# A hybrid encoder on one core: the second hyena's filters move from attention into a feed-forward layer

## The chip, the cores and the metric

The program runs on one core of one Trainium2 chip. The metric is device time in microseconds (us), the median of the runs shown. TensorE is called PE, VectorE DVE, ScalarE ACT, GpSimd POOL and SyncE SP, as in the profile.

## What is computed

An encoder of four layers over 512 tokens of 1024 channels. Each layer adds a mixer and then a gated feed-forward network to the residual `x`; the mixers are hyena, window attention, pool, hyena.

```python
for i in range(DEPTH):                      # 4
    kind, s = i % N_MIXERS, i // N_MIXERS   # hyena, attention, pool, hyena
    h = rmsnorm(x, norm_mix[i])
    ...
    x = x + y
    x = x + swiglu(rmsnorm(x, norm_ffn[i]), ff_w_gate[i], ff_w_up[i], ff_w_down[i])

def hyena_filters(L, w1, b1, wi, bi, w3, freq):
    ...                                     # h: sine layers of the positions
    h = h @ w3.astype(f32)
    h = h.reshape(L, 2, HY_ORDER, D) * decay[:, None, None, :]
    fwd, bwd = h[:, 0], h[:, 1]
    k = jnp.concatenate([fwd, jnp.zeros((1, HY_ORDER, D), f32), bwd[1:][::-1]], axis=0)
    return k / jnp.sum(jnp.abs(k), axis=0, keepdims=True)

def window_attention(xn, w_qkv, q_gain, k_gain, sink, w_o, rel_table):
    ...                                     # 16 heads, 4 key heads, blocks of 128, 3 blocks seen
    logits = jnp.where(mask[None, :, None, None], logits + bias, -1e30)
    m = jnp.maximum(jnp.max(logits, axis=-1, keepdims=True), sink_l)
    pr = jnp.exp(logits - m)
    pr = pr / (jnp.sum(pr, axis=-1, keepdims=True) + jnp.exp(sink_l - m))
    o = jnp.einsum('bnkgqs,bnskd->bnqkgd', pr.astype(vw.dtype), vw)
    return o.reshape(B, L, N_HEADS * HEAD_DIM) @ w_o
```

The filters depend on positions and weights alone, not on `x`, so those of the second hyena (layer 3) can be made at any time before it.

## The kernel before, in words

The residual lies channel-major, eight tiles `x` of 128 channels by 512 tokens. Every projection splits both operands into a high and a low part in fp32r and adds three matmuls of 512 columns (`mm3`, lines 206 to 208). `wload` fetches a weight block of 512 KB on SP's queue into `raw`; ACT makes its high part (`hi`, line 191) and DVE the rest (`lo`, line 192), with two `raw` and five `hi` and `lo` buffers.

PSUM has two pools: `mm`, four tiles of one bank, and `aux`, two tiles of two banks. A feed-forward layer (`ffn`) makes 22 blocks of hidden channels, two at a time: the gate sums in `mm`, the up sums in `aux`; then the down projection in two halves of eleven weight blocks, each half with four sums.

A hyena filter is made for an order `o` and 256 channels `q`, eight tiles for a hyena. `filter_time` multiplies the sine features by `w3` (lines 388, 389), by the decay, and takes absolute values; `filter_spectrum` makes the odd part of a discrete transform (line 430), the norm and the tap at time zero in `filter_norm` (lines 413 to 417), then the even part (line 440), joins them, and stores the tile to DRAM (`kd`, lines 450, 451), where the second hyena reads it. `filters` is a generator that yields after each piece. The first hyena's are made among its input projections.

Attention (`attention`) has 32 units: a key head, a block of 128 queries, two of its four heads. `qkv` makes the queries, keys and values in three groups; normalised queries are transposed by PE into `aux` tiles (line 834) and split. For each unit `scores` makes the products of queries and keys (lines 891, 892), adds the bias and takes the maximum on DVE (line 894), and the exponential on ACT (line 902); `turn` transposes (line 915) and copies (`pr`, line 917); `mix_values` multiplies by the values (line 928) and scales (line 930); `put_values` transposes the result back (line 936). The loop holds three units in flight, and between units takes a piece or two of `filters(1, ...)`.

A scheduler sets the final order on each engine from the order of the code, from priorities, and from when buffers of the pools come free; each engine then runs its instructions in that order.

## Time and profile before

| what | us |
|---|---|
| median of 3 runs | 2426.8 (2426.11 to 2430.69) |
| profiled execution | 2429.84 |
| its span | 2428.1 |
| PE busy in it | 2365.2 (97%) |
| DVE busy | 1446.8 (60%) |
| ACT busy | 978.2 (40%) |

The profiled execution is one of its own; what it takes beyond its span lies outside the records. Matmuls overlap in the records, so PE's busy time is not its work: distances from start to start show that. The attention units stand between 817.6 us (first scores) and 992.2 us (first matmul of the output projection); the feed-forward layer after the pool mixer fills 1440 to 1790 us and a little on both sides.

### The profile page before, as it was taken

To read this page: it belongs to the slowest core of one execution; us is meant where nothing else is said; L and a number is where in the kernel's file an instruction comes from. 1 tells how busy PE (TensorE), PEld (TensorE's weight loads), DVE (VectorE), ACT (ScalarE), POOL (GpSimd) and SP (SyncE) were. 2 spreads that over 40 slices of the span, in tenths; PEclk is the share of its full clock that TensorE was granted. 3 is DMA by queue.
4 is the path that set the end of the run, shared out by engine and by line. 5 is a ranking of instruction groups with operands and counts; after the bars stand their busy time and mean duration, and the time that the engine had idled before them with its cause. 6 is when DMAs were issued, how large, how long until landed. Compare 5 with 4: busy or idle time off the path is not lost.

```text
span 2428.1 us, 29260 instructions
## 1 busy us (share of the span) xinstructions
PE 2365.2 (97%) x10966; PEld 1951.1 (80%) x10966; DVE 1446.8 (60%) x2411; ACT 978.2 (40%) x1793; POOL 76.9 (3%) x210
## 2 busy tenths in 40 slices
PE   7999989999999899999999989999989999999999
PEld 5778878878887778888888878888878888888887
DVE  7879886454335798554443365544349997544432
ACT  6543325333234677443332363333234443333321
POOL 0210000000001021000000000000000000000000
PEclk9999999999999899999999999999999999999999
DMA  5342223433334132233332222332232222333332
GB/s 155 130 165 87 96 70 95 110 96 96 96 96 117 57 111 83 91 93 99 100 96 96 86 90 89 101 97 96 96 129 97 96 90 76 96 98 100 97 106 85
DMA packets 176833, 240.42 MB, mean 99 GB/s; under 512 B 8097, under 2 KB 137137, under 8 KB 174516
## 3 DMA queue, kind: packets, MB, share of 16 engines
q1 hardware_dynamic: 174852, 234.27, 30.0%
q0 software_dynamic: 1840, 4.29, 1.0%
q8 instruction: 86, 1.41, 0.2%
q14 instruction: 55, 0.45, 0.1%
HBM read 218.51 MB, written 20.02 MB: 98 GB/s over the span
## 4 chain that ended last, share of the span: by engine, by line
PE 60%; ACT 1%; DVE 1%; issue 0%; ACTq 0%
PE mm L206 10%; PE mm L207 10%; PE mm L208 10%; PE aux L208 7%; PE aux L207 7%; PE aux L206 7%; PE aux L711 1%; PE aux L662 1%; PE mm L928 1%; PE aux L708 1%; PE mm L999 0%; PE aux L430 0%; PE mm L634 0%; PE aux L440 0%; PE aux L653 0%; PE aux L654 0%
## 5 line engine op out<-in xcount | busy, mean ns | idle before, releaser
L192 DVE TENSOR_TENSOR lo<-raw,hi 128x512 fp32r<-128x512 f32 x700 | 483.3, 691 | 705.4 <-ACT hi L191 701.6
L191 ACT CAST hi<-raw 128x512 fp32r<-128x512 f32 x700 | 434.7, 622 | 1013.5 <-PE mm L207 647.6
L206 PE MATMUL mm<-ghs,hi 128*128 128x512 f32 x1168 | 460.8, 396 | 4.2 <-ACT ghs L517 4.2
L208 PE MATMUL mm<-ghs,lo 128*128 128x512 f32 x1168 | 460.3, 394 | 0.0
L207 PE MATMUL mm<-gls,hi 128*128 128x512 f32 x1104 | 435.4, 394 | 0.0
L208 PE MATMUL aux<-ghs,lo 128*128 128x512 f32 x704 | 274.3, 390 | 1.1 <-DVE lo L192 1.1
L206 PE MATMUL aux<-ghs,hi 128*128 128x512 f32 x704 | 274.3, 390 | 0.0
L207 PE MATMUL aux<-gls,hi 128*128 128x512 f32 x704 | 273.9, 389 | 0.0
L206 PEld LDWEIGHTS mm<-ghs,hi 128*128 128x128 f32 x1168 | 220.7, 189 | 54.2 <-ACT ghs L517 4.8
L208 PEld LDWEIGHTS mm<-ghs,lo 128*128 128x128 f32 x1168 | 220.1, 188 | 46.0 <-issue 1.2
L207 PEld LDWEIGHTS mm<-gls,hi 128*128 128x128 f32 x1104 | 208.2, 189 | 45.1 <-issue 2.5
L208 PEld LDWEIGHTS aux<-ghs,lo 128*128 128x128 f32 x704 | 132.1, 188 | 30.2 <-DVE lo L192 2.9
L207 PEld LDWEIGHTS aux<-gls,hi 128*128 128x128 f32 x704 | 132.2, 188 | 27.4
L206 PEld LDWEIGHTS aux<-ghs,hi 128*128 128x128 f32 x704 | 132.2, 188 | 27.1
L206 PE MATMUL mm<-hh,hi 128*128 128x512 f32 x352 | 137.0, 389 | 0.0
L208 PE MATMUL aux<-hh,lo 128*128 128x512 f32 x352 | 137.0, 389 | 0.0
L207 PE MATMUL mm<-hl,hi 128*128 128x512 f32 x352 | 137.0, 389 | 0.0
L206 PE MATMUL aux<-hh,hi 128*128 128x512 f32 x352 | 136.9, 389 | 0.0
L208 PE MATMUL mm<-hh,lo 128*128 128x512 f32 x352 | 136.9, 389 | 0.0
L207 PE MATMUL aux<-hl,hi 128*128 128x512 f32 x352 | 136.9, 389 | 0.0
L296 DVE TENSOR_TENSOR t<-aux,rstd 128x512 f32<-128x512 f32 x88 | 60.5, 687 | 61.9 <-PE aux L208 61.9
L300 ACT CAST hh<-t 128x512 fp32r<-128x512 f32 x88 | 54.6, 620 | 103.2 <-DVE t L297 103.1
(272 smaller groups left out, 3440.5 us busy)
## 6 DMA issues: line engine op xcount, KB each, us to landing
raw<-in_ff_w_gate SPq DMA_DIRECT2D x88, 512.0 KB
raw<-in_ff_w_up SPq DMA_DIRECT2D x88, 512.0 KB
raw<-in_ff_w_down SPq DMA_DIRECT2D x88, 512.0 KB
raw<-in_hy_w_in SPq DMA_DIRECT2D x48, 512.0 KB
kd<-k SPq DMA_DIRECT2D x32, 512.0 KB
kt<-kd SPq DMA_DIRECT2D x16, 1024.0 KB
raw<-in_hy_w_out SPq DMA_DIRECT2D x16, 512.0 KB
raw<-in_at_w_qkv SPq DMA_DIRECT2D x12, 512.0 KB
```

The source lines that it names most:

```text
L191: nc.scalar.copy(hi, raw[:, k:k + step])
L192: nc.vector.tensor_tensor(lo, raw[:, k:k + step], hi.bitcast(F32), op=ALU.subtract)
L206: mm(ps, ah, bh, start=first, stop=False)
L207: mm(ps, ah, bl, start=False, stop=False)
L208: mm(ps, al, bh, start=False, stop=last)
L296: nc.vector.tensor_tensor(t2, u[e], rstd, op=ALU.mult)
L300: nc.scalar.copy(a, t2)
L662: mm(ps[:, j, e], fwd[:, e, r0 + j], u[:, r0 + j], start=e == 0, stop=e == 1)
L708: mm(y[:, r], w, v, start=st, stop=sp)
L711: mm(y[:, e, r * P:(r + 1) * P], v[:, e * P:(e + 1) * P], w, start=st, stop=sp)
L928: nc.tensor.matmul(out, prs[j][:, b * P:(b + 1) * P], self.v[:, k, g * HD:(g + 1) * HD], start=b == 0, stop=b == len(kb) - 1)
```

## The change

The second hyena's filters are no longer made in attention. A new generator, `late_filters`, makes them for 128 channels at a time, 16 half-tiles in place of 8 tiles, and yields six times for each. The feed-forward layer with index 2 (after the pool mixer) takes one piece after each of the gate and up weight blocks from the second pair of hidden blocks on, and three pieces after each block of the down projection. Their sums stand in `mm` tiles of one bank, and half a tile is stored at a time. In attention the scores of a unit's two heads take the two banks of one `aux` tile instead of two `mm` tiles, and of the two copies in `turn` the second goes to DVE.

```diff
@@ -271,6 +271,7 @@
         self.gx_split(lambda k: self.g_ffn(i, k))
         with self.tc.tile_pool(name=f"ffn{i}", bufs=2) as fp, self.tc.tile_pool(name=f"side{i}", bufs=1) as sp:
             side = self.early(sp) if i == 0 else iter(())
+            late = self.late_filters(1, sp) if i == 2 else iter(())
             hh, hl = [], []
             for j in range(0, NF, 2):
                 g = [self.tl(self.mm, [P, L], "mm") for _ in range(2)]
@@ -284,6 +285,8 @@
                                 c = slice(e * P, (e + 1) * P)
                                 self.mm3(ps[e], ws[k][0][:, c], ws[k][1][:, c], self.gh[k0 + k], self.gl[k0 + k],
                                          k0 + k == 0, k0 + k == KD - 1)
+                        if j:
+                            next(late, None)
                 if j == 0:
                     rstd = self.rstd_row(nc.vector)
                 else:
@@ -311,8 +314,9 @@
                     for k, j in self.order(2, 4, half == 1 and k0 + 2 == NF):
                         c = slice(j * P, (j + 1) * P)
                         a, b = hh[k0 + k], hl[k0 + k]
-                        st, sp = k0 + k == 0, k0 + k == NF - 1
-                        self.mm3(ps[j], ws[k][0][:, c], ws[k][1][:, c], a, b, st, sp)
+                        self.mm3(ps[j], ws[k][0][:, c], ws[k][1][:, c], a, b, k0 + k == 0, k0 + k == NF - 1)
+                    for _ in range(3):
+                        next(late, None)
                 with self.tc.high_priority(offset=XP):
                     for j in range(4):
                         xk = self.x[4 * half + j]
@@ -487,6 +491,91 @@
                 yield
             yield from pieces(self.filter_spectrum(fp, s, o, q, *made, fwd, neg))
             made = nxt
+            yield
+
+    def late_filters(self, s, fp):
+
+        nc, t = self.nc, self.t
+        n = GS // 2
+        one = lambda tag, shape, dt=F32, bufs=1: self.tl(fp, shape, tag, dt, bufs)
+        fwd, neg = one("fwd", [P, 2, R, P]), one("neg", [P, 2, P])
+        nc.sync.dma_start(neg, t["dft_neg"])
+        nc.sync.dma_start(fwd, t["dft_fwd"])
+        C, S = lambda r: fwd[:, 0, r], lambda r: fwd[:, 1, r]
+        odd = [[[(C(1), 1), (C(3), 3)], [(S(1), 1), (S(3), 3)]],
+               [[(neg[:, 0], 1), (S(3), 3)], [(C(1), 1), (neg[:, 1], 3)]]]
+        wl = one("w3l", [P, 2, n], F32R)
+        nc.gpsimd.memset(wl[FW:P].bitcast(F32), 0.0)
+        w3 = t["hy_f_w3"][s].rearrange("p (b c) -> p b c", b=2)
+        hh = self.hh[s]
+        for q in range(NG):
+            for o in range(2):
+                self.kd[s, o, q] = self.dr.tile([P, 4, 2, GS], F32, tag=f"kd{s}{o}{q}", name=f"kd{s}{o}{q}")
+        for q, e, o in [(q, e, o) for q in range(NG) for e in range(2) for o in range(2)]:
+            c0 = q * GS + e * n
+            if o == 0:
+                dec = one("dec", [P, R, n])
+                nc.sync.dma_start(dec, t["decay"][:, :, c0:c0 + n])
+            wf = one("w3", [P, 2, n])
+            for d in range(2):
+                nc.sync.dma_start(wf[d * FW:(d + 1) * FW], w3[:, :, o * D + c0:o * D + c0 + n])
+            fb = one("fb", [1, n])
+            nc.sync.dma_start(fb, t["hy_f_bias"][s, o:o + 1, c0:c0 + n])
+            ws = one("w3s", [P, 2, n])
+            nc.vector.tensor_tensor(ws[:, 0], wf[:, 0], wf[:, 1], op=ALU.add)
+            nc.vector.tensor_tensor(ws[:, 1], wf[:, 0], wf[:, 1], op=ALU.subtract)
+            wh = one("w3h", [P, 2, n], F32R)
+            nc.scalar.copy(wh, ws)
+            nc.vector.tensor_tensor(wl[0:FW], ws[0:FW], wh[0:FW].bitcast(F32), op=ALU.subtract)
+            yield
+            ab = one("ab", [P, R, 2, n])
+            mx = one("mx", [P, 2, n])
+            for r0 in (1, 0):
+                ps = self.tl(self.mm, [P, 2, 2, n], "mm")
+                for j in range(2):
+                    c = slice((2 * j + r0) * P, (2 * j + r0 + 1) * P)
+                    nc.tensor.matmul(ps[:, j], hh[:, c], wh, start=True, stop=False)
+                    nc.tensor.matmul(ps[:, j], hh[:, c], wl, start=False, stop=True)
+                nc.vector.tensor_tensor(ab[:, r0::2], ps, dec[:, r0::2].unsqueeze(2).broadcast_to([P, 2, 2, n]), op=ALU.mult)
+                if not r0:
+                    t0 = one("t0", [1, n])
+                    nc.vector.tensor_tensor(t0, ab[0:1, 0, 0], ab[0:1, 0, 1], op=ALU.add)
+                    nc.scalar.mul(ab[0:1, 0], t0.unsqueeze(1).broadcast_to([1, 2, n]), 0.5)
+                ax = one("k4", [P, 2, 2, n], bufs=2)
+                nc.scalar.activation(ax, ab[:, r0::2], AF.Abs)
+                dst = mx if r0 else ax[:, :, 0]
+                nc.vector.tensor_tensor(dst, ax[:, :, 0], ax[:, :, 1], op=ALU.max)
+                yield
+            nc.gpsimd.tensor_tensor(mx, mx, dst, op=ALU.add)
+            nc.gpsimd.tensor_tensor(mx[:, 0], mx[:, 0], mx[:, 1], op=ALU.add)
+            po = self.tl(self.mm, [P, 2, 2, n], "mm")
+            for ty in range(2):
+                for d in range(2):
+                    for m, (w, r) in enumerate(odd[ty][d]):
+                        nc.tensor.matmul(po[:, ty, d], w, ab[:, r, d], start=m == 0, stop=m == 1)
+            od = one("k4", [P, 2, 2, n], bufs=2)
+            nc.scalar.copy(od, po)
+            yield
+            pn = self.tl(self.mm, [P, L], "mm")
+            nc.tensor.matmul(pn[:, n:n + 1], mx[:, 0], self.ones, start=True, stop=True)
+            nc.vector.reciprocal(self.rn[s][q][:, o, e:e + 1], pn[:, n:n + 1])
+            nc.tensor.matmul(pn[0:1, :n], self.ones, mx[:, 0], start=True, stop=True)
+            tap = one("t0", [1, n])
+            nc.vector.tensor_tensor(tap, pn[0:1, :n], fb, op=ALU.mult)
+            nc.vector.tensor_tensor(ab[0:1, 0, 0], ab[0:1, 0, 0], tap, op=ALU.add)
+            yield
+            pe = self.tl(self.mm, [P, 2, 2, n], "mm")
+            for j in range(2):
+                for d in range(2):
+                    nc.tensor.matmul(pe[:, j, d], fwd[:, d, 2 * j], ab[:, 2 * j, d], start=True, stop=True)
+            e2 = one("e2", [P, 2, n])
+            nc.scalar.copy(e2, pe[:, 1])
+            ka, kb = ab[:, 0:2], ab[:, 2:4]
+            nc.vector.tensor_tensor(ka[:, 0], pe[:, 0], e2, op=ALU.add)
+            nc.vector.tensor_tensor(ka[:, 1], pe[:, 0], e2, op=ALU.subtract)
+            nc.vector.tensor_tensor(kb, ka, od, op=ALU.subtract)
+            nc.vector.tensor_tensor(ka, ka, od, op=ALU.add)
+            nc.sync.dma_start(self.kd[s, o, q][:, :, :, e * n:(e + 1) * n], ab)
             yield
 
 
@@ -747,8 +836,6 @@
                 nc.gpsimd.memset(kl[HD:P].bitcast(F32), 0.0)
             ol = [self.tl(a1, [P, 2, L], "ol", F32R)] + qs[0:3]
             self.ol = [a[:, e] for a in ol for e in range(2)]
-            fwd = self.tl(a1, [P, 2, R, P], "fwd")
-            neg = self.tl(a1, [P, 2, P], "neg")
             units = [(g, n, e) for g in range(NKV) for n in range(NB) for e in range(2)]
             made, put = {}, {}
             with ExitStack() as inner:
@@ -760,10 +847,6 @@
                     for _ in self.qkv(i, qp, a1):
                         for j in range(2):
                             made[j] = self.scores(ap, *units[j])
-                fp = inner.enter_context(self.tc.tile_pool(name="fil1", bufs=2))
-                steps = self.filters(1, fp, fwd, neg, 0)
-                for _ in range(2):
-                    next(steps)
                 n = len(units)
                 for j in range(n + 3):
                     if 2 <= j < n:
@@ -774,10 +857,6 @@
                         made[j - 1] = self.turn(ap, *made[j - 1])
                     if 0 <= j - 3:
                         self.put_values(*units[j - 3], put.pop(j - 3))
-                    for _ in range(5 * (j + 1) // 4 - 5 * j // 4):
-                        next(steps, None)
-                for _ in steps:
-                    pass
             self.project(t["at_w_o"][0], self.gh, self.ol, self.natural)
 
     def qkv(self, i, ap, a1):
@@ -845,6 +924,7 @@
         if not self.ready:
             self.ready = True
             yield from self.bias_rows(pool)
+            self.rn[1] = [self.tl(self.per, [P, 2, GS // P], f"rn1{q}") for q in range(NG)]
             yield from self.filter_features(pool, self.per, self.mm, 1)
 
     def bias_rows(self, pool):
@@ -885,8 +965,9 @@
         bias = self.bias[g][e]
         m = self.tl(ap, [P, 4], "m", bufs=4)
         s = []
+        both = self.tl(self.aux, [P, 2, L], "aux")
         for j in range(2):
-            ps = self.tl(self.mm, [P, L], "mm")
+            ps = both[:, j]
             q, k = self.q[h0 // 2][:, j, n * P:(n + 1) * P], (g // 2, g % 2)
             nc.tensor.matmul(ps[:, :w], q, self.kh[k[0]][:, k[1], k0:k0 + w], start=True, stop=False)
             nc.tensor.matmul(ps[:, :w], q, self.kl[k[0]][:, k[1], k0:k0 + w], start=False, stop=True)
@@ -914,7 +995,7 @@
             for b in range(len(kb)):
                 nc.tensor.transpose(pt[:, b * P:(b + 1) * P], s[j][:, b * P:(b + 1) * P], self.ident)
             pr = self.tl(ap, [P, 3 * P], "pr", bufs=4)
-            nc.scalar.copy(pr[:, :w], pt[:, :w])
+            (nc.vector.tensor_copy if j else nc.scalar.copy)(pr[:, :w], pt[:, :w])
             pts.append(pt)
             prs.append(pr)
         return kb, pts, prs, den
```

Outside attention's units and this feed-forward layer the order on every engine is as before. Three places follow. A row is a line of the code (the changed kernel has its own numbers), the instruction, out<-in with buffer numbers, and its size; "x2" merges rows.

**The start of attention, PE.** `qh` are normalised queries (their transposes go to `aux`), `kh`, `kl` and `q` keys and queries in scores. Before:

```order
L834 MATMUL aux_1235_6271<-ident_16_87,qh1_1232_6262 128x128
L834 MATMUL aux_1236_6282<-ident_16_87,qh1_1232_6262 128x128
L936 MATMUL mm_1297_6499<-ident_16_87,o_1278_6432 128x128
L891 MATMUL mm_1305_6528<-kh0_1068_5516,q0_1064_5512 128x384
L892 MATMUL mm_1305_6528<-kl0_1070_5518,q0_1064_5512 128x384
L928 MATMUL mm_1293_6487<-v_1063_5511,pr_1294_6491 128x64 x3
L928 MATMUL mm_1295_6493<-v_1063_5511,pr_1296_6497 128x64
L834 MATMUL aux_1235_6271<-ident_16_87,qh2_1233_6265 128x128
L834 MATMUL aux_1236_6282<-ident_16_87,qh2_1233_6265 128x128
L928 MATMUL mm_1295_6493<-v_1063_5511,pr_1296_6497 128x64 x2
L834 MATMUL aux_1235_6271<-ident_16_87,qh3_1234_6268 128x128
```

Now, the last of the transposes on PE and what follows them:

```order
L913 MATMUL aux_1238_6304<-ident_16_87,qh0_1231_6259 128x128
L913 MATMUL aux_1238_6304<-ident_16_87,qh1_1232_6262 128x128
L913 MATMUL aux_1238_6304<-ident_16_87,qh2_1233_6265 128x128
L913 MATMUL aux_1238_6304<-ident_16_87,qh3_1234_6268 128x128
L972 MATMUL aux_1244_6328<-kh0_1072_5520,q0_1068_5516 128x384
L973 MATMUL aux_1244_6328<-kl0_1074_5522,q0_1068_5516 128x384
L972 MATMUL aux_1255_6364<-kh0_1072_5520,q1_1069_5517 128x384
L973 MATMUL aux_1255_6364<-kl0_1074_5522,q1_1069_5517 128x384
```

The scores of the third unit (384 columns, `q0`) and of later ones stood ahead of and among the 32 transposes of the last four query tiles; now all 32 stand ahead of the third unit.

**Inside attention, PE.** `w3h`, `w3l`, `ab` and `mx` belong to the filters, `lg` and `pr` to `turn` and `mix_values`. Before:

```order
L388 MATMUL aux_1337_6637<-w3h_1321_6582,hh_814_4084 128x512
L389 MATMUL aux_1337_6637<-w3l_1243_6324,hh_814_4084 128x512
L891 MATMUL mm_1416_6907<-kh0_1068_5516,q2_1066_5514 128x384
L892 MATMUL mm_1416_6907<-kl0_1070_5518,q2_1066_5514 128x384
L430 MATMUL aux_1355_6700<-ab_1260_6377,fwd_1073_5523 128x256 x4
L430 MATMUL aux_1355_6700<-ab_1260_6377,neg_1074_5524 128x256
L430 MATMUL aux_1355_6700<-ab_1260_6377,fwd_1073_5523 128x256 x2
L430 MATMUL aux_1355_6700<-ab_1260_6377,neg_1074_5524 128x256
L413 MATMUL aux_1370_6754<-ones_9_80,mx_1268_6403 128x1 x2
```

Now, on PE at such a place, there are units alone:

```order
L996 MATMUL mm_1371_6779<-ident_16_87,lg_1354_6713 128x128 x3
L972 MATMUL aux_1389_6840<-kh0_1072_5520,q2_1070_5518 128x256
L973 MATMUL aux_1389_6840<-kl0_1074_5522,q2_1070_5518 128x256
L996 MATMUL mm_1373_6785<-ident_16_87,lg_1355_6717 128x128 x3
L1017 MATMUL mm_1375_6791<-ident_16_87,o_1358_6728 128x128
L972 MATMUL aux_1377_6796<-kh0_1072_5520,q3_1071_5519 128x384
L973 MATMUL aux_1377_6796<-kl0_1074_5522,q3_1071_5519 128x384
L1009 MATMUL mm_1371_6779<-v_1067_5515,pr_1372_6783 128x64 x3
L1009 MATMUL mm_1373_6785<-v_1067_5515,pr_1374_6789 128x64 x3
```

The filter matmuls are gone, and about one pair of scores and one result's transpose stand between a unit's transposes and its products with the values.

**The down projection, PE and DVE.** `hh` and `hl` are hidden blocks, `hi` and `lo` weight parts. Before, PE had projection matmuls alone:

```order
L206 MATMUL aux_2756_13230<-hh6_2533_12103,hi_2775_13337 128x512
L207 MATMUL aux_2756_13230<-hl6_2534_12104,hi_2775_13337 128x512
L208 MATMUL aux_2756_13230<-hh6_2533_12103,lo_2776_13338 128x512
L206 MATMUL mm_2757_13231<-hh6_2533_12103,hi_2775_13337 128x512
L207 MATMUL mm_2757_13231<-hl6_2534_12104,hi_2775_13337 128x512
L208 MATMUL mm_2757_13231<-hh6_2533_12103,lo_2776_13338 128x512
```

Now, at the same place on PE, a half-tile's tap sum (1x128) and even spectrum (`fwd`) stand among them; its norm stands two matmuls ahead of these rows:

```order
L562 MATMUL mm_2722_13248<-mx_2709_13179,ones_9_80 1x128
L206 MATMUL aux_2687_13077<-hh6_2380_11633,hi_2732_13282 128x512
L207 MATMUL aux_2687_13077<-hl6_2381_11634,hi_2732_13282 128x512
L208 MATMUL aux_2687_13077<-hh6_2380_11633,lo_2733_13283 128x512
L206 MATMUL mm_2688_13078<-hh6_2380_11633,hi_2732_13282 128x512
L570 MATMUL mm_2724_13255<-ab_2708_13178,fwd_2263_11059 128x128 x4
```

On DVE there stand at this place (`rn11` is the norm, `t0` the tap, `ab` what the even spectrum reads):

```order
L547 TENSOR_TENSOR k4_2714_13198<-k4_2714_13198 128x2x128
L561 RECIPROCAL rn11_707_3563<-mm_2722_13248 128x1
L192 TENSOR_TENSOR lo_2760_13417<-raw_2758_13414,hi_2759_13416 128x512
L564 TENSOR_TENSOR t0_2723_13252<-mm_2722_13248,fb_2700_13136 1x128
L565 TENSOR_TENSOR ab_2708_13178<-ab_2708_13178,t0_2723_13252 1x128
L574 TENSOR_TENSOR ab_2708_13178<-mm_2724_13255,e2_2725_13260 128x256
```

Four projection matmuls lie between the tap sum (1x128) and the even spectrum, which reads the sum of `ab` and the tap; a weight split stands on DVE between the norm and the tap. Ten of the 16 half-tiles lie in the down projection in this way; the other six lie among the gate and up blocks, with 22 matmuls at that point.

## Rows read from the trace of the kernel before

**Rows 1.** The page: busy us by engine; one costly group, with its mean ns.

```profile
PE 2365.2 (97%) x10966; PEld 1951.1 (80%) x10966; DVE 1446.8 (60%) x2411; ACT 978.2 (40%) x1793; POOL 76.9 (3%) x210
...
L192 DVE TENSOR_TENSOR lo<-raw,hi 128x512 fp32r<-128x512 f32 x700 | 483.3, 691 | 705.4 <-ACT hi L191 701.6
```

**Rows 2.** Windows: stretch, busy us (count) by engine, clock, DMA share, GB/s.

```profile
100.00:150.00 50.00, 49.72 (x227) 39.23 (x226) 44.76 (x65) 26.93 (x45) 9.56 (x18) 1.00 0.34 124
817.60:842.00 24.40, 18.55 (x92) 16.43 (x90) 16.25 (x57) 19.18 (x49) 0.00 (x0) 0.72 0.07 22
852.00:992.20 140.20, 133.94 (x827) 112.61 (x827) 118.85 (x346) 104.64 (x310) 26.42 (x34) 1.00 0.28 96
1440.00:1790.00 350.00, 349.72 (x1551) 289.39 (x1550) 151.50 (x235) 112.36 (x185) 0.00 (x0) 1.00 0.31 96
```

**Rows 3.** Timeline of PE in attention: start, duration, instruction.

```profile
903.08 0.28 PE L892 MATMUL mm<-kl,q 128*128 128x256 f32 x1
903.20 0.28 PE L891 MATMUL mm<-kh,q 128*128 128x256 f32 x1
...
922.32 0.33 PE L892 MATMUL mm<-kl,gls 128*128 128x384 f32 x1
922.49 0.34 PE L891 MATMUL mm<-kh,gls 128*128 128x384 f32 x1
```

**Rows 4.** Chain of work in attention: start, time on the chain, pieces merged.

```profile
961.93 2.21 PE aux L430 x10
...
967.41 0.36 PE aux L413 x4
...
977.57 1.28 PE mm L928 x12
978.86 0.66 PE mm L915 x6
```

**Rows 5.** Timeline of PE in the first hyena, transforms among projection matmuls.

```profile
317.03 1.05 PE L711 MATMUL aux<-inv,c 128*128 128x128 f32 x8
317.84 0.47 PE L207 MATMUL mm<-zl,hi 128*128 128x512 f32 x1
318.15 0.39 PE L208 MATMUL mm<-zh,lo 128*128 128x512 f32 x1
...
322.48 0.60 PE L711 MATMUL aux<-inv,c 128*128 128x128 f32 x4
322.84 0.48 PE L206 MATMUL mm<-zh,hi 128*128 128x512 f32 x1
323.15 0.40 PE L207 MATMUL mm<-zl,hi 128*128 128x512 f32 x1
```

**Rows 6.** Groups of PE by line, 852.0 to 992.2 us: count, busy us.

```profile
L430 PE MATMUL aux<-ab,fwd 128*128 128x256 f32 x96 | 24.1, 382 | 0.0
...
L388 PE MATMUL aux<-w3h,hh 128*128 128x512 f32 x32 | 13.5, 431 | 0.4 <-ACT w3h L380 0.2
```

**Rows 7.** Timeline of DVE and PE in attention, from the tap to its use.

```profile
968.65 0.41 DVE L417 TENSOR_TENSOR t<-aux,fb 1x256 f32<-1x256 f32 x1 [0.62 <-PE aux L415]
...
969.10 0.63 DVE L439 TENSOR_TENSOR ab<-ab,t 1x256 f32<-1x256 f32 x1
...
969.72 0.38 PE L440 MATMUL aux<-ab,fwd 128*128 128x256 f32 x1
```

**Rows 8.** Timeline of DVE and ACT at the start of attention.

```profile
831.07 4.91 DVE L827 TENSOR_TENSOR qh<-q,rs_r 128x512 f32<-128x512 f32 x8
...
839.05 2.18 ACT L839 ACTIVATE gls<-aux,vec 128x1024 fp32r<-128x1024 f32 x2 [0.69 <-PE aux L834]
...
841.35 2.50 DVE L840 SCALAR_TENSOR_TENSOR gls<-aux,vec,gls 64x1024 fp32r<-64x1024 f32 x2
```

**Rows 9.** Timeline of PE at the end of attention, one row a unit.

```profile
984.35 0.27 PE L936 MATMUL mm<-ident,o 128*128 128x128 f32 x1
...
987.36 0.27 PE L936 MATMUL mm<-ident,o 128*128 128x128 f32 x1
```

## The prediction

> **What bounds the kernel now.** First the page's busy times: TensorE (PE) is busy 97% of the span [rows 1], so a change pays only where it removes PE work or PE waiting. Then the busy time by stretch [rows 2]: the reader is to see that the feed-forward layer after the pool mixer (1440 to 1790 us) is full, 349.72 of 350.00 us, while attention has two parts. From 817.6 to 842.0 us the PE is busy 18.55 of 24.40 us at a mean granted clock of 0.72 of full (a mixture of its two levels, 1.2 and 2.4 GHz). From 852.0 to 992.2 us it is busy 133.94 of 140.20 us at full clock, with VectorE (DVE) at 118.85 and ScalarE (ACT) at 104.64. So inside attention the filters fill a PE that attention alone would leave waiting now and then, and in the feed-forward layer there is nothing to fill. The change carries PE work from the one to the other. Everything outside these two stretches stands in the same order on every engine.
>
> Busy time counts overlapping matmuls, so I price PE work by start-to-start distance. The 512-column matmuls of the feed-forward layer are 350 / 1551 = 0.226 us apart [rows 2]; a 256-column one in fp32r takes 0.12, a 384-column one 0.17 [rows 3]; a record of a plain fp32 matmul (the trace has two records for each) 0.22 at 256 columns, 0.107 at 64 columns, 0.09 at one, and a transpose 0.11 [rows 4]. For fp32 records of 128 columns put between projection matmuls: 8 of them take 0.81 us and the next matmul 0.31 instead of 0.226, 0.91 in all with the short rest; 4 of them take 0.36 and the next again 0.31, 0.46 in all [rows 5]. So a record costs about 0.10 and each change between the two kinds about 0.1.
>
> **What leaves attention.** By the code each of the eight filter tiles has 8 fp32r matmuls of 512 columns (four at each of two lines; 32 records at L388 [rows 6]), 8 + 4 plain ones of 256 columns for the spectra (the 96 records at L430 [rows 6] are six of these per tile, twice), one of 256 columns for the tap sum and two of one column: 64 x 0.226 + 208 x 0.22 + 32 x 0.09 = 63 us, before changes of kind.
>
> **What enters the feed-forward layer.** 16 half-tiles instead of 8 tiles. Each has 8 fp32r matmuls of 256 columns (0.92), 16 records of 128 columns in one group (1.61 + 0.1 = 1.71), 2 one-column records (0.2 + 0.1), 2 of 128 columns (0.2 + 0.1) and 8 of 128 columns (0.91): 4.14 us, so 66 us for 16. Halving the columns is nearly free in streaming: two records of 128 columns (0.20) replace one of 256 (0.22), two fp32r matmuls of 256 (0.24) one of 512 (0.226). The Trainium skill says in "Perfetto Trace Analysis", section Matmuls, that larger matmuls are more efficient than smaller ones; by that rule, were a halved matmul to cost as much as a whole one, the pieces would take 2 x 63 = 126 us instead of 66, and the kernel 2502. The rows show that only the changes of kind grow, by some 3 us; I go by the rows.
>
> To this come waits. In the down projection ten half-tiles have only four projection matmuls (0.9 us) between the tap sum and the spectrum matmuls that need the tap, and DVE has a split of a weight tile, 0.69 us [rows 1], ahead of the tap product (second and third places under the change). In the trace of before the tap product starts at 968.65, the addition at 969.10, and the spectrum matmul that needs it at 969.72: 1.07 us [rows 7]; before the product lies the tap sum itself, some 0.3 us. With halved rows I take 1.3 us, of which 0.9 is covered: 0.4 x 10 = 4 us. Bounds: 0 where DVE is early, 1.5 x 10 = 15 where the split always stands in front. Together the layer grows by **70 us** (64 if changes of kind overlap; 82 with the larger wait).
>
> What else moves is covered. SP's queue gets 16 filter stores and 58 small loads among the weight loads; a store waits for its last DVE product, and the weight loads behind it wait too, but by the order weight tiles are split two blocks (48 matmuls, 11 us) ahead of their use. DMA engines are busy 0.31 there, and 0.28 in attention with all its transfers and the filters' [rows 2]: both together over 420 us stay at 0.35. DVE is busy 151.50 and ACT 112.36 of 350 us, in attention 118.85 and 104.64 of 140 [rows 2]: were all of that to move, they would be at 0.64 and 0.52 of 420 us. In the first layer's stretch with the same mixture of filters and projections the PE loses 0.28 of 50 us with DVE at 44.76 [rows 2]; that cover gone, each late split would stop the PE by up to its 0.69 us. The POOL additions leave attention's queue, where the bias loads stand, and nothing waits for those.
>
> **What attention gives back.** Without filters its units must fill the PE by themselves. A unit of two-block windows costs 4 x 0.12 + 4 x 0.11 + 8 x 0.107 + 0.11 = 1.9 us, one of three blocks 4 x 0.17 + 6 x 0.11 + 12 x 0.107 + 0.11 = 2.7 us. Two or three score groups of fp32r lie among plain fp32 records, so 0.35 us of changes of kind each.
>
> The start decides when they begin. The scores now take the two-bank sums that the query transposes also take, and in the new order 32 transposes of the last four query tiles stand ahead of the third unit's scores (first place under the change); today four more units' scores stand ahead of or among these. The transposes wait for the normalised queries (4.91 us of DVE from 831.07 [rows 8]); I put these 1.5 us earlier than now, an estimate, since the third unit's work no longer runs beside that chain. Then four tiles pass through two buffers, each with 1.1 us on ACT and 1.25 us on DVE [rows 8], and release one for the third unit at about 842. From there 30 units: 14 x 1.9 + 16 x 2.7 + 30 x 0.35 = 80 us. Filling and draining the chain (scores, maximum, exponential, transpose, product) adds some 4.5 us, with the half-rate clock of the idle start in it. Last, waits in each unit: at today's tail, where little filter work is left, two units of two blocks are 3.01 us apart [rows 9] with 2.25 us of their own and about 0.4 of a filter, so 0.35 us of waits. 842 + 80 + 4.5 + 10.5 = 937 for the end, instead of 992.2: attention gives back **55 us**. Bounds: 65 without any waits, 41 with 0.8 us in every unit. The second copy of a pair moved from ACT to DVE shortens ACT's part; neither engine is the bound, so I give it nothing by itself.
>
> **Sum.** 70 - 55 = +15 us. The profiled execution took 2429.84 us (span 2428.1 and 1.7 around it), so it would take about 2445; it lies 3 us above the median of the runs, 2426.8, so I expect 2442 for the median.
>
> **Rivals.** One: nothing to be measured. Attention runs with no waits (65) and the layer takes 66: 2428. For it: the new PE order keeps about 1 us of other work between a transpose and its product; against it: today's units wait even with filters to fill in.
>
> Two: faster. The start closes up: the PE's 24.4 us there hold about 8 us of work for two units and the transposes, so 16 us lie idle or at half clock. If scores that no longer wait for the projection's four sums bring the transposes forward by 12 us, and units run with no waits, attention gives back 77 us: 2416. It decides from an end of attention before 917 us. Against it: the transposes wait for the query chain on ACT and DVE, which the change leaves alone.
>
> Three: much slower. In the layer DVE takes instructions in order; where a filter product that waits for the PE stands before a weight split, the PE waits for the split. One such stop of 1.2 us in each of the 16 half-tiles beyond my 4 us: the layer grows by 89, 2461. The Trainium skill's section Optimization Strategy in "Perfetto Trace Analysis" recommends interleaving regimes whose most contended engine differs; by that rule the filters stood well beside attention and stand badly beside a layer that is bound by the same PE, and its outcome is the forecast itself or this rival.
>
> **How the numbers follow.** A measurement of this kernel tells 0.2% (5 us) from no change. Chances: forecast (2432 to 2452) 0.62; rival one (2422 to 2432) 0.14; rival two 0.08; rival three, with its milder forms (above 2452), 0.16. So faster 0.08, same 0.14, slower 0.78. The bounds alone give 64 - 65 = -1 to 82 - 41 = +41, 2426 to 2468; I give 2425 to 2460, which leaves out most of rival two and the worst of rival three.
>
> **What would show it.** Right: the layer after the pool mixer 70 us longer, PE full in it, filter records at the same distances as above; attention's first projection matmul near 937 with PE busy share under 0.9 in its units; the third unit's scores near 842. Wrong: that matmul before 925, or the layer grown by less than 62 us, would give no change or a gain; PE idle in the layer with a DVE releaser, or PE clock under full within attention's units, would put it above my range.

## The result, and the profile after

The changed kernel takes 2458.6 us (median of 4 runs, 2458.0 to 2459.0) against 2428.6 for the kernel before: a ratio of 1.0118, interval [1.0106, 1.0130]. It is slower by 30 us, where the forecast was 2442, slower by 15. The direction was right and the time lies at the upper edge of the range, but the increase is twice the one forecast. The profiled execution took 2458.0 us with a span of 2456.0, 27.9 us more than the span before.

Three distances of the trace split these 27.9 us. From the first gate matmul to the last matmul of the feed-forward layer after the pool mixer it was 1422.09 to 1794.36, 372.3 us; now it is 1362.04 to 1820.89, 458.9 us: the layer grew by **86.6 us** (forecast 70). The layer begins **60.05 us** earlier: attention gave that back (forecast 55). What follows the layer comes 1.4 us later still. 86.6 - 60.05 + 1.4 = 27.9, but for rounding. The last term does not come with the filters alone: with the same filters in the layer it is 0.1 us in the trace of e2 and 0.4 in that of e3 (both below), where the granted clock behind the layer was that of before (last section).

First the page of the changed kernel: busy times, then the chain that ended last, by engine and by line; the answer to [rows 1].

```profile
PE 2378.6 (97%) x11238; PEld 1961.2 (80%) x11238; DVE 1470.1 (60%) x2563; ACT 975.3 (40%) x1809; POOL 81.0 (3%) x226
...
PE 59%; DVE 2%; DMA 2%; ACT 2%; issue 1%; POOL 0%; POOLq 0%; DVEq 0%; ACTq 0%
PE mm L206 10%; PE mm L208 10%; PE mm L207 10%; PE aux L208 7%; PE aux L207 7%; PE aux L206 7%; DMA kd<-ab 2%; PE mm L1009 1%; PE aux L800 1%; PE aux L751 1%; PE aux L797 1%; PE mm L555 1%; PE aux L972 1%; PE mm L570 1%; PE mm L996 1%
```

TensorE (PE) is still at 97%, and yet the reader should stop at one entry: a DMA, the store of the filter spectra from the tile `ab` to `kd`, stands on the chain with 2% of the span (nine landings, 41 us in all). Transfers that nobody waits for are not on a chain.

Next the busy time by stretch, columns as in [rows 2]: attention from its third unit's scores to its projection; the layer's gate and up phase; its down projection; the start of the hyena behind it.

```profile
844.70:932.40 87.70, 81.40 (x608) 72.91 (x609) 62.46 (x302) 71.12 (x273) 10.54 (x20) 0.96 0.09 24
1410.00:1644.40 234.40, 234.40 (x1144) 195.54 (x1143) 134.71 (x250) 86.19 (x155) 10.25 (x14) 1.00 0.37 108
1644.40:1821.00 176.60, 166.43 (x867) 133.56 (x865) 91.56 (x195) 59.22 (x108) 11.30 (x18) 1.00 0.35 104
1820.00:1850.00 30.00, 22.65 (x87) 18.15 (x86) 19.43 (x35) 13.90 (x29) 2.99 (x12) 0.77 0.44 157
```

Attention's units are better filled than I thought (81.40 of 87.70 us). The gate and up phase is full, with 40 of the 96 filter pieces in it. The down projection, which holds the other 56, loses 10.2 of 176.6 us; this phase was full before the change, as the whole layer was [rows 2]. So the page's 97% hides a local loss. The waits of PE in the layer say for whom (instruction, what it waited for, us in total, times, longest):

```profile
PE mm L560 <- POOL mx L550: 6.0, 9, 1.3
PE mm L555 <- DVE ab L539: 4.0, 6, 1.8
```

L560 is the norm sum (one column), the first matmul that needs the maxima that POOL adds up; the tap sum (L562) stands two projection matmuls behind it in most half-tiles. Where an expectation below has a wait "before the tap sum", it is this one. L555 is the odd spectrum, which needs the first decay product in `ab`. Counted from the moment when the next matmul usually starts (0.227 us after the last one), the two cost 7.5 and 5.6 us, 13.1 together. The waits of DVE in the down projection name what is behind them:

```profile
DVE ab L539 <- DMA kd<-ab: 13.0, 8, 3.3
```

How this reaches PE is seen in the chain of work through one half-tile (start, time on the chain, what):

```profile
1656.52 4.87 DMA kd<-ab
...
1661.41 0.04 DVE ab L539
...
1662.02 0.68 DVE lo L192
...
1663.22 0.41 DVE mx L547
...
1663.86 0.42 ACT ab L543
...
1664.31 0.64 ACT k L545
...
1664.97 0.44 DVE k L547
...
1665.57 0.75 POOL mx L549
...
1666.38 0.46 POOL mx L550
...
1666.89 0.38 PE mm L560 x2
```

Read it downwards. The store of the half-tile before is issued at 1656.52 and lands 4.87 us later. `ab` has one buffer, so the next half-tile's first product (L539) cannot start before. DVE was free for it 1.92 us earlier. From there the two products (with a weight split, L192, between them), absolute values, maxima and POOL's two additions follow one another with no long gap and end at 1666.84; the norm sum (L560) starts at 1666.89. The rows of that product and of the odd spectrum, 0.41 us late for it, in the timeline (the idle time before each and what ended it in brackets):

```profile
1661.41 0.69 DVE L539 TENSOR_TENSOR ab<-mm,dec 128x512 f32<-128x512 f32 x1 [1.92 <-DMA kd<-ab]
...
1662.25 0.46 PE L555 MATMUL mm<-ab,fwd 128*128 128x128 f32 x2 [0.41 <-DVE ab L539]
```

### The profile page after: what moved, and what is told of

Its sections match the earlier page's. It is cut to its first block, busy times and chain, and to the rows that moved or that the text cites. A ratio compares the mean times of both kernels' runs of the same rounds, so it can differ in the third digit from the quotient of the medians.

```text
span 2456.0 us, 30081 instructions
## 1 busy us (share of the span) xinstructions
PE 2378.6 (97%) x11238; PEld 1961.2 (80%) x11238; DVE 1470.1 (60%) x2563; ACT 975.3 (40%) x1809; POOL 81.0 (3%) x226
## 4 chain that ended last, share of the span: by engine, by line
PE 59%; DVE 2%; DMA 2%; ACT 2%; issue 1%; POOL 0%; POOLq 0%; DVEq 0%; ACTq 0%
PE mm L206 10%; PE mm L208 10%; PE mm L207 10%; PE aux L208 7%; PE aux L207 7%; PE aux L206 7%; DMA kd<-ab 2%; PE mm L1009 1%; PE aux L800 1%; PE aux L751 1%; PE aux L797 1%; PE mm L555 1%; PE aux L972 1%; PE mm L570 1%; PE mm L996 1%
## 5 line engine op out<-in xcount | busy, mean ns | idle before, releaser
L192 DVE TENSOR_TENSOR lo<-raw,hi 128x512 fp32r<-128x512 f32 x700 | 483.4, 691 | 630.9 <-ACT hi L191 618.8
L207 PE MATMUL mm<-gls,hi 128*128 128x512 f32 x1104 | 436.1, 395 | 0.0
L207 PE MATMUL aux<-gls,hi 128*128 128x512 f32 x704 | 274.4, 390 | 0.0
L207 PEld LDWEIGHTS mm<-gls,hi 128*128 128x128 f32 x1104 | 208.6, 189 | 44.4 <-issue 2.5
L207 PEld LDWEIGHTS aux<-gls,hi 128*128 128x128 f32 x704 | 132.3, 188 | 26.5
L207 PE MATMUL aux<-hl,hi 128*128 128x512 f32 x352 | 138.3, 393 | 0.0
L207 PE MATMUL mm<-hl,hi 128*128 128x512 f32 x352 | 138.1, 392 | 0.0
```

Of the source, the lines that this page charges most:

```text
L192: nc.vector.tensor_tensor(lo, raw[:, k:k + step], hi.bitcast(F32), op=ALU.subtract)
L207: mm(ps, ah, bl, start=False, stop=False)
```

## The experiments

Times are medians; the kernel before took 2430.4 us beside e1 to e4, 2429.6 beside e5 to e8 and 2430.5 beside e9 to e12.

**e1, a second buffer for the store.**

```
-            ab = one("ab", [P, R, 2, n])
+            ab = one("ab", [P, R, 2, n], bufs=2)
-                    t1 = self.tl(fp, [P, L], "t1")
+                    t1 = self.tl(fp, [P, L], "t1", bufs=1 if i == 2 else 2)
-                    t2 = self.tl(fp, [P, L], "t2")
+                    t2 = self.tl(fp, [P, L], "t2", bufs=1 if i == 2 else 2)
```

> The filter buffer that the store reads (ab) gets a second copy; room for it comes from two feed-forward scratch tiles of that layer. In the changed kernel the PE idles 13 us in the down projection at two places: 5.6 before the odd spectrum, which waits for the first decay product, and 7.5 before the tap sum, which waits for the maxima on POOL. Theory A (the buffer's reuse: the first product waits until the store of the half-tile before has landed, 3.5 to 6.3 us after its issue, and drags all that follows): with the new order of the pieces (4 projection matmuls instead of 16 before the odd spectrum, 20 instead of 9 before the tap sum) both waits go but for some 0.3 us a half-tile, so 2447 to 2450 instead of 2458.6. Theory B (the store stands in SP's queue ahead of weight loads): nothing changes, 2457 to 2459. Theory C (DVE's order, weight splits ahead of the products, the forecast's third rival): the products are as late as before and stand nearer to their users, 2458 to 2462.

Measured: 2444.9 us, ratio to before 1.0059 [1.0044, 1.0074]. The two waits are gone entirely; the down projection's window reads:

```profile
1646.00:1810.00 164.00, 163.97 (x867) 134.18 (x865) 90.57 (x196) 60.13 (x113) 11.28 (x18) 1.00 0.39 115
```

The layer takes 445.9 us, 12.9 less than in the changed kernel. Theories B and C fall. The order moved too, but it does not explain the gain: the odd spectrum lost cover (4 projection matmuls instead of 16 after the products) and the norm sum has as much as before in all (24 instead of 25).

**e2, another spread of the same pieces.**

```
                         if j:
-                            next(late, None)
+                            for _ in range(2 if k0 else 1):
+                                next(late, None)
...
-                    for _ in range(3):
+                    for _ in range(2):
```

> Six pieces instead of four go into each pair of gate and up blocks and two instead of three into each down block, so ten half-tiles lie in the gate and up phase and six in the down projection. In the changed kernel the six half-tiles in the gate and up phase cost the PE no wait, those in the down projection 1.4 us each. Theory A (store to reuse): a half-tile in the down projection now spans three blocks, 16.3 us of projections instead of 10.9, so the store has one block more and has landed; waits of 13 us shrink to under 3: 2447 to 2450. Theory B and theory C (a cost per half-tile of the down projection whatever the distance): 6 x 1.4 = 8.4 us of waits stay, 2453 to 2455.

Measured: 2450.2 us, 1.0082 [1.0067, 1.0097]. At the edge of theory A's forecast; the waits of PE in the layer show why it is not better:

```profile
PE aux L206 <- ACT hi L191: 3.3, 9, 0.4
PE aux L208 <- DVE lo L192: 1.5, 9, 0.2
PE mm L561 <- POOL mx L551: 0.7, 1, 0.7
```

Of the waits at the two old places 0.7 is left: distance to the store cures the wait as a second buffer does. But with two pieces between the same projection blocks a new wait stands in the gate and up phase, nine times: PE waits for the casts and splits of weight tiles, 4.8 us in all. It is not the mechanism of my third rival. The cast ahead of one of these stops had itself waited for PE (`aux` L207), and ahead of the split DVE had a product of the feed-forward layer (L300), not one of the filters:

```profile
1474.94 0.62 ACT L191 CAST hi<-raw 128x512 fp32r<-128x512 f32 x1 [2.10 <-PE aux L207]
```

**e3, the store from another queue.**

```
-            nc.sync.dma_start(self.kd[s, o, q][:, :, :, e * n:(e + 1) * n], ab)
+            nc.scalar.dma_start(self.kd[s, o, q][:, :, :, e * n:(e + 1) * n], ab)
```

> The 16 stores are issued by ACT instead of SP. Theory A: the store lands as late as before and the first product waits for it as before; 2456 to 2461. Theory B (SP's queue holds the weight loads behind a store that waits for DVE): the down projection's waits of 13 us go, 2446 to 2449; were it ACT that then blocks, the casts of the weight tiles behind the store would come late and it would be slower than 2461.

Measured: 2459.7 us, 1.0121 [1.0104, 1.0138], as theory A has it. The two waits only trade places:

```profile
PE mm L555 <- DVE ab L539: 9.9, 8, 1.4
PE mm L560 <- POOL mx L550: 2.2, 3, 1.1
```

DVE still waits for the landing of the store (19.5 us in nine waits, where it was 13.0 in eight). SP's queue is not the cause.

**e4, no second filters.** `late = iter(())`, and the second hyena reads `self.rn[0]` and `self.kd[0, o, g]`.

> The second hyena's filters are left out altogether: it uses the first hyena's filter spectra and norms instead, so the output is another one; all else is the changed kernel. This weighs the two sides apart. By the traces the layer took 372.3 us without and 458.9 with the filters and the hyena that follows starts 1.4 us later, so 2458.6 - 87 to 88 = 2371, with 58 us below the kernel before: attention's give-back. By the forecast's own sizes (70 and 55) it would be 2389 and 2374.

Measured: 2370.6 us, 0.9754 [0.9739, 0.9768]. So attention gives back 59.8 us, and the filters cost 88 us where the change puts them, by run times and without any reading of a trace.

**e5, e1 without the tap sum.**

```
-            nc.tensor.matmul(pn[0:1, :n], self.ones, mx[:, 0], start=True, stop=True)
...
-            nc.vector.tensor_tensor(tap, pn[0:1, :n], fb, op=ALU.mult)
+            nc.vector.tensor_tensor(tap, fb, fb, op=ALU.mult)
```

> The kernel with two filter buffers (2444.9 us, no PE wait left in the layer), without the tap sum's two row records: the tap is made from the bias alone, so the filters are not the reference's. It sizes the second error, the half-tile's own cost: 73.7 us for 16 where the forecast had 66. By the rows of that kernel the two records and the longer distances after them take 0.63 us a half-tile: 10 us less, 2434 to 2436. By the forecast's 0.3 us it would be 2440, and the missing 8 us would lie elsewhere.

Measured: 2436.1 us, 1.0027 [1.0017, 1.0036], 8.8 below e1 (8 by the two ratios), where the forecast's own size gives 4.8. These are the rows in e1, PE's timeline (start, duration, instruction):

```profile
1667.58 0.40 PE L207 MATMUL aux<-hl,hi 128*128 128x512 f32 x1
1667.90 0.38 PE L562 MATMUL mm<-mx,ones 128*1 128x128 f32 x2
1668.21 0.50 PE L208 MATMUL aux<-hh,lo 128*128 128x512 f32 x1
1668.55 0.40 PE L206 MATMUL aux<-hh,hi 128*128 128x512 f32 x1
1668.79 0.39 PE L207 MATMUL aux<-hl,hi 128*128 128x512 f32 x1
```

The two records L562 push the next matmul to 0.63 us after the last one, and the one behind that comes 0.34 instead of 0.227 later. Less two usual distances that is 0.41 + 0.11 = 0.52 us (in the expectation I had counted the last 0.11 twice), 8.4 for 16. I had taken 0.30, from records that write 128 rows; these write a single row.

**e6, one-bank scores in the changed kernel.**

```
-        both = self.tl(self.aux, [P, 2, L], "aux")
         for j in range(2):
-            ps = both[:, j]
+            ps = self.tl(self.mm, [P, L], "mm")
```

> The changed kernel with the scores' sums in two single banks again, shared with the transposes, as before the change; the filters stay in the feed-forward layer. It asks what gives attention's 60 us back. Theory D (attention's own PE work and the leaving filters): 2456 to 2462. Theory E (the two-bank sums: with four single banks for scores and transposes together a unit waits for the unit before): 0.3 to 0.8 us for each of 30 units, 2468 to 2483.

Measured: 2456.7 us, 1.0112 [1.0095, 1.0129]. Theory D: the two-bank sums give nothing back. The copy on DVE stays in this run, so what it is worth without filters is not shown. The run shows another thing: its third unit's scores start at 822.02 us, 22.7 earlier than in the changed kernel, and yet attention takes 112.5 us from its first scores to its projection instead of 114.4. The start of the third unit is not what decides the end.

**e7 and e8, the small parts alone, filters left in attention.** e7 is e6's edit in reverse on the kernel before, and e8's edit with it; e8 is this alone:

```
-            nc.scalar.copy(pr[:, :w], pt[:, :w])
+            (nc.vector.tensor_copy if j else nc.scalar.copy)(pr[:, :w], pt[:, :w])
```

> The kernel before, filters in attention, with only the small parts of the change: scores in two-bank sums and the second pair's copy on DVE. The filters' spectra use the same two-bank sums. PE idled 6.3 of 140 us there. Theory D: at most these come back, 2423 to 2431. Theory E': the scores now queue for the two buffers behind the filters' spectra, 2433 to 2445.

> The kernel before with only the second pair's copy moved from ACT to DVE. ACT has 104.6 and DVE 118.9 us of 140 busy in attention, neither is the bound: 2427 to 2432, no difference. If DVE's fuller queue delays the filters' products it is 2433 or more; if ACT's copies hold the transposes back now, 2420 to 2425.

Measured: e7 2462.7 us, 1.0134 [1.0119, 1.0149], beyond every forecast; e8 2440.8 us, 1.0044 [1.0029, 1.0059], slower where I expected nothing, though I had named 2433 or more should DVE's fuller queue delay the filters' products. Beside filters the small parts are harmful, and without them (e6) the sums are neutral. In e8 the projection starts at 1002.46 instead of 992.20, and from 842 to 992 us PE is busy 138.27 us instead of 141.66, DVE 135.84 instead of 127.90 (first the kernel before, then e8):

```profile
842.00:992.00 150.00, 141.66 (x887) 119.44 (x886) 127.90 (x374) 112.68 (x334) 28.36 (x37) 1.00 0.28 95
842.00:992.00 150.00, 138.27 (x846) 113.75 (x844) 135.84 (x381) 98.92 (x285) 28.36 (x37) 1.00 0.27 91
```

**e9, the store in long pieces.** The spectra's tile becomes `[P, 2, 4, 2, n]`, stored as `self.kd[s, o, q][:, e]`, and loaded by halves.

> The changed kernel with one filter buffer as it was, but the spectra lie in DRAM by half-tiles, so a store writes 4 KB in one piece for each partition instead of eight pieces of 512 B; the hyena reads each spectrum in two loads. Theory A (the landing of the store sets the wait) by its size: if long pieces land sooner, by some 1.5 us of 4.9, the two waits shrink by 9 x 1.5 = 13 us at most: 2446 to 2452. If the landing time hangs on the 512 KB and the weight tile issued just ahead, it lands as late and the time stays, 2456 to 2460.

Measured: 2456.9 us, 1.0112 [1.0098, 1.0126]. The landing does not change; the chain of that kernel has for the first two stores of the down projection:

```profile
1655.41 4.90 DMA kd<-ab
1672.24 4.95 DMA kd<-ab
```

**e10, e11, e12, attempts on the kernel before.** e10 takes the sums `w3s` to `nc.gpsimd` for the second hyena, e11 the last sum `ka + od`; e12 has `range(6)` for `range(2)` ahead of attention's loop.

> The kernel before with the second hyena's filters' two sums of weights (7.4 us of DVE in attention's 150) on POOL instead. Adding the copy of a pair to DVE in attention (about 12 us) had made the kernel before 11 us slower. Theory F (in attention DVE's queue paces the filters' products): 3 to 7 us faster, 2422 to 2427. Theory G (only that copy's place between transpose and product mattered): 2427 to 2432.

> The kernel before with the last sum of each filter tile (9.7 us of DVE in attention's 150) on POOL instead; the store then waits for POOL, nothing else does. Theory F: 4 to 9 us faster, 2420 to 2426. Theory G: 2427 to 2432. If POOL takes more than some 3 us for each and holds up the maxima behind it, 2433 or more.

> The kernel before with six instead of two filter pieces ahead of attention's third unit. In the 24.4 us of the start the PE was busy 18.6 at a mean clock of 0.72. If more filter work fits between the query chain's waits there: up to 8 us faster, 2420 to 2426. If the pieces cannot run there, because their tiles come free only when the query tiles do, or DVE is held by the query chain: 2427 to 2432.

Measured: e10 2430.9 us, 1.0000 [0.9992, 1.0009]; e11 2429.6 us, 0.9999 [0.9990, 1.0008]; e12 2436.1 us, 1.0024 [1.0015, 1.0033]. Theory F's gain does not come, but these two runs do not test it, for DVE's load did not fall. The same window in e10, then in e11:

```profile
842.00:992.00 150.00, 140.75 (x883) 118.99 (x882) 127.70 (x358) 113.22 (x334) 41.36 (x53) 1.00 0.29 97
842.00:992.00 150.00, 140.78 (x883) 118.96 (x882) 126.65 (x363) 111.63 (x333) 47.10 (x45) 1.00 0.28 98
```

DVE has 16 and 11 instructions fewer here and is busy 127.70 and 126.65 us, where it was 127.90. From 817 us to the projection, where all of the moved sums lie, it is busy 145.7 and 144.5 us, 144.6 before: what left came back in the durations of other rows. In e11 the 16 sums of weights take 10.1 us instead of 7.4. Why they lengthen is not shown, and whether a lighter DVE would gain there stays untested. Early pieces harm. No version tried beats the kernel before.

## Why the prediction was wrong by half

**The failed step** is the sentence "What else moves is covered", in what it says of SP's queue. I asked what stands behind a waiting store on SP and how busy the DMA engines are on the mean, and not who waits until the store has landed. The diff showed both ends: the spectra are stored out of `ab`, and `one("ab", ...)` takes one buffer. The price is the landing, 4.87 us, less the 2.97 (in that half-tile) from the store's issue to the moment when DVE could have begun the product; I read neither the landing of such a store from the trace of before nor that distance from the order. The sum has 4 us for all waits in the layer; 13.1 were measured, and with the second buffer (e1) they vanish. The DMA engines' mean share was 0.35 as forecast, and it says nothing of one transfer's landing: six stores in the down projection with a weight tile of the same size issued 0.6 us ahead landed in 4.79 to 6.25 us, three with none issued in the 2.3 us ahead in 3.50 to 3.52. One of each, SP's issues first, then the two landings on the chain:

```profile
1655.91 0.37 SPq L185 DMA_DIRECT2D raw<-in_ff_w_down  x1
1656.52 0.58 SPq L578 DMA_DIRECT2D kd<-ab  x1
...
1756.52 0.37 SPq L185 DMA_DIRECT2D raw<-in_ff_w_down  x1
...
1763.26 0.57 SPq L578 DMA_DIRECT2D kd<-ab  x1
```

```profile
1656.52 4.87 DMA kd<-ab
...
1763.26 3.52 DMA kd<-ab
```

The Trainium skill ("SBUF — State Buffer", section The DMA setup-cost knee) fits a transfer by about 2 us whatever the size plus the bytes at 436 GB/s, an estimate of 3.2 us for 512 KB; the row without a weight tile just ahead, 3.52, lies a tenth above it, and that of the store behind a weight tile does not fit the rule for a single transfer. The Trainium skill also says ("Trainium Kernel Development and Optimization", section Quick Reference, Key Constraints) that DMAs from the queues of SP, ACT and POOL run on the same 16 DMA engines, so that another issuer saves issue time only; e3 agrees, with no gain.

**The wait that I did price** was the wrong one. The 4 us between the tap and the even spectrum did not occur: the spectrum's first matmul follows the projection matmul ahead of it at the usual distance in all ten half-tiles of the down projection, and so it does in e1, where nothing ahead of it is late. From the tap sum's start to the spectrum the order itself has 1.34 us (1667.76 to 1669.10); I had set 1.3 us of need, the tap sum's own time in it, against the 0.9 of the projection matmuls alone. (The upper bound was also added up wrongly: 66 + 15 is 81, not 82.)

**The own cost of the half-tiles** was 73.7 us, read from e1's layer (445.9 - 372.3), where I had 66. Of the 7.7 us the tap sum's one-row records make 0.22 x 16 = 3.5 (e5). The odd spectrum takes 1.79 us in the gate and up phase and 1.99 in e1's down projection instead of 1.71, about 3 more. The norm sum's records cost 0.23 instead of 0.30, which gives back about 1. The rest, between 1 and 2 us, is spread over projection matmuls behind the pieces, 0.23 to 0.235 apart instead of 0.227. The products of 256 columns (0.96 for 0.92) and the even spectrum (0.90 for 0.91) came nearly as forecast.

**Attention's side** was right in kind, and 5 us too small. The third unit's scores and the first projection matmul:

```profile
844.72 0.45 PE L972 MATMUL aux<-kh,q 128*128 128x384 f32 x1 [0.82 <-DVE gls L919]
...
932.40 0.48 PE L206 MATMUL mm<-ghs,hi 128*128 128x512 f32 x1
```

The start came 2.7 us later than forecast (844.7 for 842), the 30 units took 87.7 instead of 95. PE's busy time of 81.4 is close to the 80 that I counted; its idle time is 6.3 us, where I had given 4.5 to filling and 10.5 to waits in the units. The sign "PE busy share under 0.9 in its units" was wrong: it is 0.93. The sign "PE clock under full" came (0.96 over the units) and did not put the time above the range. The term that was argued wrongly is "The start decides when they begin": in e6 the third unit starts at 822.02 and the end hardly moves.

**The sum**, forecast and measured: half-tiles 66 and 73.7; waits 4 and 13.1; give-back 55 and 60.05; behind the layer 0 and 1.4. So 15 and 28. With 13.1 of waits and my own other terms it would have been 24. The waits are the largest miss (9.1), the halves' own cost the next (7.7), and the attention that gave back 5 more than forecast hides part of both.

**The rivals.** One and two are out: attention closed up, but the layer grew by 86.6, not 66. Three has almost the measured time (2461) by another mechanism: in the changed kernel PE waits for filter products, and for the split of a weight tile only 0.3 us, as before the change. No run shows its mechanism; e2's stops come nearest. The Trainium skill ("Perfetto Trace Analysis", section Optimization Strategy) says that interleaving regimes with different most contended engines may improve performance, and I gave that as the reason why the filters stood well in attention. The windows from attention's first scores to its projection, before and after, show little of it:

```profile
817.60:992.20 174.60, 160.29 (x978) 135.97 (x976) 144.16 (x430) 131.92 (x382) 28.36 (x37) 0.96 0.25 86
818.00:932.40 114.40, 96.88 (x673) 84.45 (x672) 78.40 (x342) 85.27 (x302) 10.54 (x20) 0.88 0.09 23
```

PE's busy time falls by 63.4 us and its idle time grows from 14.3 to 17.5: the filters had filled 3.2 us of gaps. Of the 13.5 us between their own cost in the layer (73.7) and what attention gives back by these windows (60.2), about 10 are PE time that the halves cost more than the whole tiles did. No run put whole tiles into the layer. So the second buffer does not save this move: without waits it still loses some 14 us, as e1 shows.

**Open** is why the copy on DVE costs 11 us beside the filters (e8). e10 and e11 do not answer it, since DVE's busy time did not fall in them. The order of all engines changed with each; I have not separated that.

## What to carry to other kernels

When a change stores straight out of a work tile, find who writes that tile next and set the time between them against the transfer's landing, with the transfer issued just ahead of it; mean DMA load says nothing of that. Weigh a move by the work at both ends before any wait: work that is cut finer at its new place costs more there, and how much its old place gives back is read from the idle time that it leaves. And a stretch at full share elsewhere proves nothing for its neighbour: one piece every 24 projection matmuls ran free, three every 24 stalled. When work is moved off an engine, look whether the engine's busy time fell.

## What the runs showed of the hardware

A store of 512 KB landed in 3.5 us, and in 4.8 to 6.3 us behind a weight tile of 512 KB issued 0.6 us ahead. Whether it wrote pieces of 512 B or of 4 KB made no difference (4.87 and 4.92 us against 4.90 and 4.95 for the first two stores of the down projection, e9). Two fp32 records that write one row of 128 columns cost 0.52 us among fp32r matmuls, where four that write 128 rows cost 0.46 [rows 5]. Behind the layer PE idled 3.65 us before eight one-column matmuls in both kernels; they took 1.05 us before and 1.86 after the change, and the mean granted clock of the 30 us from the layer's end was 0.83 before and 0.77 after. It is 0.83 also in e2 and e3, with the filters in the layer and the same 3.65 us of idling, so the filters alone do not bring it. Moving 7.4 or 9.7 us of sums from DVE to POOL (e10, e11) left DVE's busy time in attention as it was, while POOL's rose by 13 and 19 us.
